# One pool of eight PSUM banks in place of a pool of three and a pool of five, in a one-core decoder layer

## The chip, the cores and the metric

The kernel runs on one core of one Trainium2 chip. The metric is the device time of one execution in microseconds. Before the change it was measured three times: 2459.76, 2463.95 and 2460.2 us, a median of 2460.2 us. One more execution was recorded by the hardware profiler; the profile and every answer of the trace come from that one.

The engines are named as in the profile: PE is TensorE's matmul (PEld its weight load), DVE is VectorE, ACT is ScalarE, POOL is GpSimd, SP is SyncE, which issues most DMAs.

## The reference, cut to what matters

One decoder layer over a prompt of 2048 tokens and 8 single-token samples, model width 1024, in float32:

```
mod  = silu(c) @ w_ada + b_ada                      # shift, scale, gate, twice
h    = rmsnorm(x, g_mix) * (1 + scale_m) + shift_m
q, k, v, g_ret, x_lru, g_lru = split(h @ w_in)      # 3072 columns
ret  = silu(g_ret) * groupnorm(retention(rotary(q), rotary(k), v))   # 4 heads of 128
lru  = rg_lru(causal_conv4(x_lru)) * gelu(g_lru)    # 512 channels
x    = x + gate_m * (concat(ret, lru) @ w_out)
h    = rmsnorm(x, g_ffn) * (1 + scale_f) + shift_f
u    = causal_conv3(h @ w_up_conv)                  # 2816 columns
x    = x + gate_f * ((gelu(u) * (h @ w_up_gate)) @ w_down)
y    = rmsnorm(x, g_final)
```

Beside y, the new states of the retention, of the RG-LRU and of both convolutions are returned, for the prompt and for the samples.

## The kernel before, in words

**Groups and blocks.** The 2056 columns (tokens) are worked off in three groups of 688, 680 and 688, each cut into two blocks of 344 or 340 columns. Activations lie with the channel on the partition and the token along the row. A group runs through the whole layer before the next one's large products begin; at the seam between two groups the final norm of the one and the load and first norm of the other run side by side.

**Large products.** Every float32 product is made from a high and a low part in three matmuls (`mm3`, lines 373 to 375: high x high, high x low, low x high), all into one tile of PSUM. PSUM has eight banks in this program, and a tile takes one bank of 512 float32. Three kinds of large product exist:

- `proj` (line 605): a column block of `w_in` times the normed input, 24 matmuls into one tile. `head_item` then reads the tile with VectorE (the rotary turn, lines 622 to 624) or with ScalarE, `lru_x` and `lru_g` with ScalarE.
- `down_item` (line 845): `w_out` or `w_down`. Of `w_down` one tile takes the contributions of two feature tiles, that is six matmuls, and the last two pairs are done together with twelve. VectorE's line 851 reads the tile and adds it, times the gate, to `x`.
- `quad_item` (with `product`): the two up-projections by a scheme of seven products for a 2 x 2 block matrix (`PRODUCTS`, P1 to P7). A family of seven products uses up to three tiles, called x, z and y (`qx`, `qz`, `qy` in the profile); products of one family accumulate into the same tile after ScalarE's or VectorE's copy of what stood there before (`keep`, line 1016, high priority). In the first three pairs y comes from the pool of the large products, everything else from the other one.

**Small products.** Transposes of the input (`xT`) and of the output (`yT`, line 1118), the retention's chunks (`kvT`, `o`, `oT`), the gates of the RG-LRU (`zr`, `zi`), the modulation (`ada`) and the norms' broadcasts (`bc`, `bc2`, `z`). In `final`, a chunk of up to 128 tokens takes two `yT` tiles; ScalarE squares them (line 1120), and VectorE scales them into the output (line 1130) once the norm is known.

**Weights.** A block of weights is fetched raw, split into high and low (ScalarE line 303, POOL or VectorE line 304), and written back to memory in the first group; later groups fetch the finished parts. For the up-projections VectorE also forms sums of blocks (line 357), in the first group only. Eight blocks of weights can be held.

**What sets the order.** The program is written as a list of items in the order of need (`group_items`), with two queues of side work: `soon` (norms, RG-LRU chains, final norm) and `bg` (retention), of which a step is emitted after an item. The build then hands all of it to a planner that runs a simulated clock (`_TC`): at each engine the ready instruction with the earliest place in the program goes next, `high_priority` moves a place forward. A tile gets its bank when its first writer is placed, and an instruction that finds no bank free in its pool is left waiting while later ones go ahead. So the banks that a pool has take part in deciding the order on every engine.

**The pools of PSUM.** Pool `pm` (line 111) has three banks (`PM`, line 34) and is reached by `psm`; pool `pt` (line 112) has the other five and is reached by `pst`. From `pm` come `proj`, `down`, the early `qy`, the first group's `bc` and a few output transposes at the very end; from `pt` comes the rest.

Of the kernel before, what the change touches and what calls it, by code (L numbers as in the profile page):

```python
# [10 lines left out]
F32 = mybir.dt.float32  # L11
# [5 lines left out]
P = 128  # L17
# [13 lines left out]
WIDE, HASTE = 9, 200  # L31
SPLIT = (2, 5)
FIRST = 4
PM = 3
LAGB, LAG = 1, 2


# [61 lines left out]
def hybrid_step(ctx: ExitStack, tc: tile.TileContext, I, O):  # L99
# [8 lines left out]
    tp = ctx.enter_context(tc.tile_pool(name="t", bufs=10))  # L108
    sp = ctx.enter_context(tc.tile_pool(name="s", bufs=3))
    dp = ctx.enter_context(tc.tile_pool(name="d", bufs=1, space=bass.MemoryType.DRAM))  # L110
    pm = ctx.enter_context(tc.tile_pool(name="pm", bufs=PM, space=bass.MemoryType.PSUM))
    pt = ctx.enter_context(tc.tile_pool(name="pt", bufs=8 - PM, space=bass.MemoryType.PSUM))

    def ctile(cols, name, dt=F32):
        return con.tile([P, cols], dt, tag=name, name=name)
# [2 lines left out]
        return tp.tile([P, BMAX + 4], F32, tag="t", name=name)  # L118

    def psm(name):  # L120
        return pm.tile([P, 512], F32, tag="m", name=name)

    def pst(name):
        return pt.tile([P, 512], F32, tag="t", name=name)

    def slot(name, dt=F32):
        return xp.tile([P, 4, TMAX], dt, tag="x", name=name)
# [29 lines left out]
    V.memset(cT, 0.0)  # L157
    cTv = cT.rearrange("p (k b) -> p k b", b=32)
    ps = pst("c_ps")
    T.transpose(ps[:, 0:72], crow[0:72, :], ident[0:72, 0:72])  # L160
    th = tiny(72, "cth")
# [25 lines left out]
    def load_rows(i, t_):  # L187
        col = sum(n for g in stage[:i] for _, n in g)
        r = sum(n for _, n in stage[i])
        q = pst("rows_ps")  # L190
        T.transpose(q[:, 0:r], t_[0:r, :], ident[0:r, 0:r])
        S.activation(out=vec[:, col:col + r], in_=q[:, 0:r], func=AF.Copy)
# [186 lines left out]
    def ada_mm(j, k):  # L379
        if k == 0:  # L380
            ada_ps[j] = pst("ada")
        ada_acc(ada_ps[j], units.pop(("w_ada", j, k)), k)
        if k == KC - 1:
            ada_finish([(j, 0)], ada_ps[j])
# [89 lines left out]
    class Group:  # L474
# [83 lines left out]
        def norm1(g, b, how):  # L558
            bc = pst("bc") if g.gi else psm("bc")
            for i, (c0, w) in enumerate(g.pieces):  # L560
                a0, a1 = max(c0, b[0]), min(c0 + w, b[1])
                if a0 < a1:
                    dg = tiny(P, "dg")
                    V.tensor_scalar(out=dg[0:w, 0:a1 - a0], in0=ident[0:w, a0 - c0:a1 - c0],
                                    scalar1=g.r1[i][0:w, 0:1], scalar2=None, op0=ALU.mult)
                    T.matmul(bc[:, a0 - b[0]:a1 - b[0]], ones[0:w, :], dg[0:w, 0:a1 - a0],
                             start=True, stop=True)
            yield
            yield from g.hnorm(b, bc, 1, 0, how)
# [33 lines left out]
        def proj(g, unit, b):  # L603
            n = b[1] - b[0]
            q = psm("proj")
            for k in range(KC):
                mm3(q[:, 0:n], *unit[k], g.hh[k // 4][:, k % 4, b[0]:b[1]], g.hl[k // 4][:, k % 4, b[0]:b[1]],
                    k == 0, k == KC - 1)
            return q[:, 0:n]
# [232 lines left out]
        def down_item(g, keys, parts, jg, b, m):  # L842

            np_, n = g.npr(b), b[1] - b[0]
            q = psm("down")
            for i, key in enumerate(keys):
                wh, wl = (v[:, m % 4, :] for v in units[key])
                xh, xl = parts[i][b]
                mm3(q[:, 0:n], wh, wl, xh, xl, i == 0, i == len(keys) - 1)
            xs = g.xk(m)[:, b[0]:b[0] + np_]  # L850
            V.scalar_tensor_tensor(out=xs, in0=q[:, 0:np_], scalar=modv[:, jg, m, 0:1], in1=xs,  # L851
                                   op0=ALU.mult, op1=ALU.add)
            if np_ < n:
                if (jg, m) not in g.started:
                    g.started.add((jg, m))
                    V.tensor_copy(fsv[:, m, :], q[:, np_:n])
                else:
                    V.tensor_tensor(out=fsv[:, m, :], in0=fsv[:, m, :], in1=q[:, np_:n], op=ALU.add)
# [594 lines left out]
```

## Time and profile before

| What | us |
|---|---|
| median of three runs | 2460.2 |
| the profiled execution | 2463.86 |
| its span, first to last instruction | 2462.1 |
| PE busy in the span | 2359.8 (96%) |
| PEld busy | 2275.5 (92%) |
| DVE busy | 1452.9 (59%) |
| ACT busy | 869.6 (35%) |
| POOL busy | 716.9 (29%) |
| mean granted TensorE clock | 0.988 |

Matmuls overlap: each is shown with some 0.32 us, though one starts about every 0.16 us. A stretch without holes shows PE and PEld busy all the time, so the idle time before an instruction, and what ended it, says more than the busy share. In the view of waits a row reads: the engine and tile that waited, the instruction that ended the wait, then the total in us, the number of times, and the longest.

### The profile page before, as it was taken

How to read it: one execution, taken by the hardware profiler on the slowest of the kernel's cores; microseconds unless marked ns; L12 is line 12 of the kernel's file. 1: busy time of each engine (PE TensorE's matmuls, PEld its weight loads, DVE VectorE, ACT ScalarE, POOL GpSimd, SP SyncE). 2: the span in 40 equal slices, each digit the busy share in tenths (PEclk: the TensorE clock that was granted, in tenths of full speed). 3: DMA queues.
4: the chain of work that ended last, by engine and by line, in shares of the span. 5: the costliest groups of instructions: out<-in, count | busy, mean ns of one | idle time of the engine just before them, and what ended most of it. 6: DMA issues, size and time to landing. Idle time of an engine off the chain costs nothing.

```text
span 2462.1 us, 40114 instructions
## 1 busy us (share of the span) xinstructions
PE 2359.8 (96%) x15157; PEld 2275.5 (92%) x15157; DVE 1452.9 (59%) x3181; ACT 869.6 (35%) x1964; POOL 716.9 (29%) x739
## 2 busy tenths in 40 slices
PE   5999998999999999999899999999999989999998
PEld 4987797999999999999899999999999989999998
DVE  5646777875766665666754444446667675444444
ACT  4323554544444444243422222243124241222222
POOL 3444440257666743243001010112222210101011
PEclk9999999999999999999999999999999999999999
DMA  9476655878878875343566666666442465666674
GB/s 299 163 261 223 210 172 190 305 276 287 304 285 304 323 251 184 120 157 139 189 222 235 222 238 220 241 213 215 139 130 96 145 231 199 239 220 234 219 252 160
DMA packets 243493, 536.04 MB, mean 218 GB/s; under 512 B 19223, under 2 KB 114055, under 8 KB 243292
## 3 DMA queue, kind: packets, MB, share of 16 engines
q1 hardware_dynamic: 242220, 532.01, 62.6%
q8 instruction: 120, 1.97, 0.3%
q10 hardware_dynamic: 696, 0.91, 0.1%
q0 software_dynamic: 384, 0.56, 0.1%
q14 instruction: 73, 0.60, 0.1%
HBM read 385.10 MB, written 148.42 MB: 217 GB/s over the span
## 4 chain that ended last, share of the span: by engine, by line
PE 53%; DVE 4%; ACT 2%; DMA 1%; issue 1%; POOL 1%; POOLq 0%; SPq 0%; ACTq 0%; DVEq 0%
PE down L374 6%; PE down L373 6%; PE down L375 6%; PE qx L374 4%; PE qx L375 4%; PE qx L373 4%; PE proj L373 3%; PE proj L375 3%; PE proj L374 3%; PE qz L373 2%; PE qz L374 2%; PE qz L375 2%; PE qy L374 1%; PE qy L373 1%; PE qy L375 1%
## 5 line engine op out<-in xcount | busy, mean ns | idle before, releaser
L851 DVE SCALAR_TENSOR_TENSOR x<-down,mod,x 128x344 f32<-128x344 f32 (+2 forms) x624 | 349.0, 569 | 347.0 <-PE down L375 342.3
L373 PE MATMUL proj<-hh,wb 128*128 128x344 f32 (+1 forms) x1152 | 378.5, 329 | 14.3 <-DVE h L580 6.0
L375 PE MATMUL proj<-hh,wb 128*128 128x344 f32 (+1 forms) x1152 | 373.6, 325 | 2.7 <-POOL wb L304 2.5
L374 PE MATMUL proj<-hl,wb 128*128 128x344 f32 (+1 forms) x1152 | 372.5, 323 | 0.0
L458 POOL TENSOR_TENSOR ffl<-cv,ffh 128x344 fp32r<-128x344 f32 (+1 forms) x120 | 124.7, 1046 | 782.0 <-ACT ffh L457 736.7
L374 PE MATMUL qx<-op,wb 128*128 128x344 f32 (+1 forms) x1020 | 325.5, 319 | 2.6 <-DVE op L921 2.6
L373 PE MATMUL qx<-op,wb 128*128 128x344 f32 (+1 forms) x1020 | 324.7, 320 | 1.2 <-ACT op L920 1.2
L375 PE MATMUL qx<-op,wb 128*128 128x344 f32 (+1 forms) x1020 | 324.5, 319 | 0.0
L373 PE MATMUL down<-ffh,wb 128*128 128x344 f32 (+1 forms) x960 | 304.7, 324 | 7.6 <-DVE x L851 7.4
L375 PE MATMUL down<-ffh,wb 128*128 128x344 f32 (+1 forms) x960 | 306.4, 319 | 0.0
L374 PE MATMUL down<-ffl,wb 128*128 128x344 f32 (+1 forms) x960 | 306.3, 319 | 0.0
L304 POOL TENSOR_TENSOR wb<-wr,wb 128x512 fp32r<-128x512 f32 x164 | 223.9, 1376 | 230.7 <-ACT wb L303 222.1
L373 PEld LDWEIGHTS proj<-hh,wb 128*128 128x128 f32 x1152 | 218.4, 190 | 25.9 <-issue 9.5
L375 PEld LDWEIGHTS proj<-hh,wb 128*128 128x128 f32 x1152 | 218.7, 190 | 5.7 <-POOL wb L304 3.9
L374 PEld LDWEIGHTS proj<-hl,wb 128*128 128x128 f32 x1152 | 219.1, 190 | 3.3 <-POOL hl L588 0.9
L1076 DVE SCALAR_TENSOR_TENSOR cv<-u,vec,cv 128x344 f32<-128x344 f32 (+2 forms) x264 | 170.8, 665 | 50.6 <-ACT cv L1056 48.1
L374 PEld LDWEIGHTS qx<-op,wb 128*128 128x128 f32 x1020 | 191.7, 188 | 3.4 <-DVE op L921 3.4
L373 PEld LDWEIGHTS qx<-op,wb 128*128 128x128 f32 x1020 | 191.5, 188 | 2.0 <-ACT op L920 1.8
L373 PEld LDWEIGHTS down<-ffh,wb 128*128 128x128 f32 x960 | 179.3, 188 | 14.3 <-DVE x L851 13.7
L375 PEld LDWEIGHTS qx<-op,wb 128*128 128x128 f32 x1020 | 191.4, 188 | 0.0
L373 PE MATMUL qz<-op,wb 128*128 128x344 f32 (+1 forms) x528 | 169.7, 325 | 14.6 <-ACT op L920 10.7
L375 PEld LDWEIGHTS down<-ffh,wb 128*128 128x128 f32 x960 | 180.6, 188 | 0.0
(314 smaller groups left out, 4952.1 us busy)
## 6 DMA issues: line engine op xcount, KB each, us to landing
wb<-w_down SPq DMA_DIRECT2D x100, 512.0 KB
wb<-w_up_conv_S SPq DMA_DIRECT2D x92, 512.0 KB
wb<-w_up_gate_S SPq DMA_DIRECT2D x92, 512.0 KB
wb<-w_in SPq DMA_DIRECT2D x72, 512.0 KB
wb<-w_up_conv_A SPq DMA_DIRECT2D x69, 512.0 KB
wb<-w_up_gate_A SPq DMA_DIRECT2D x69, 512.0 KB
w_in<-wb SPq DMA_DIRECT2D x48, 512.0 KB
w_up_conv_S<-wb SPq DMA_DIRECT2D x44, 512.0 KB
```

Source lines behind the costliest of these rows:

```text
L304: lo_on.tensor_tensor(out=w[:, 512:1024], in0=src, in1=w[:, 0:512].bitcast(F32), op=ALU.subtract)
L373: T.matmul(out, wh, xh, start=first, stop=False, skip_group_check=more)
L374: T.matmul(out, wh, xl, start=False, stop=False, skip_group_check=more)
L375: T.matmul(out, wl, xh, start=False, stop=last, skip_group_check=more)
L458: G.tensor_tensor(out=lo[:, 0:n], in0=src, in1=hi[:, 0:n].bitcast(F32), op=ALU.subtract)
L851: V.scalar_tensor_tensor(out=xs, in0=q[:, 0:np_], scalar=modv[:, jg, m, 0:1], in1=xs, op0=ALU.mult, op1=ALU.add)
L1076: V.scalar_tensor_tensor(out=cv[:, 0:np_], in0=u[:, j:j + np_], scalar=cfw[:, j, ft:ft + 1], in1=cv[:, 0:np_], op0=ALU.mult, op1=ALU.add)
```

## The change

The two pools of PSUM become one pool of eight banks. `psm` and `pst` remain as names, and both take a tile from that pool, under one tag. Which tile uses which of the two names is as before, and nothing else in the program differs.

```diff
-PM = 3
...
-    pm = ctx.enter_context(tc.tile_pool(name="pm", bufs=PM, space=bass.MemoryType.PSUM))
-    pt = ctx.enter_context(tc.tile_pool(name="pt", bufs=8 - PM, space=bass.MemoryType.PSUM))
+    pb = ctx.enter_context(tc.tile_pool(name="pb", bufs=8, space=bass.MemoryType.PSUM))
...
     def psm(name):
-        return pm.tile([P, 512], F32, tag="m", name=name)
+        return pb.tile([P, 512], F32, tag="b", name=name)
 
     def pst(name):
-        return pt.tile([P, 512], F32, tag="t", name=name)
+        return pb.tile([P, 512], F32, tag="b", name=name)
```

## The prediction

> **What bounds the kernel now.** The page came first, for the engines over the whole span.
>
> ```profile
> span 2462.1 us, 40114 instructions
> PE 2359.8 (96%) x15157; PEld 2275.5 (92%) x15157; DVE 1452.9 (59%) x3181; ACT 869.6 (35%) x1964; POOL 716.9 (29%) x739
> ```
>
> TensorE sets the time: no other engine is above 59%, and what the change can win has to come out of the share in which TensorE has no work it may start. Matmul times overlap, so the weight loads (PEld) show the holes better. Which stage has them is read from the stage table, a row for each stretch: the feed-forward of the first token group (580 to 860 us), the seam behind it, the feed-forward of the second group, the next seam, the feed-forward of the third, and the tail.
>
> ```profile
> 580.00:860.00 280.00, 272.46 (x1705) 266.28 (x1704) 186.72 (x266) 130.36 (x298) 189.08 (x144) 1.00 0.82 299
> 860.00:930.00 70.00, 66.71 (x436) 64.58 (x435) 39.34 (x79) 29.39 (x73) 26.74 (x28) 0.98 0.75 267
> ...
> 1210.00:1620.00 410.00, 405.39 (x2592) 404.33 (x2592) 190.05 (x367) 114.22 (x298) 41.03 (x41) 1.00 0.67 232
> 1620.00:1700.00 80.00, 75.84 (x500) 74.39 (x500) 43.43 (x95) 28.24 (x68) 19.06 (x22) 0.98 0.63 218
> ...
> 1990.00:2400.00 410.00, 405.72 (x2567) 404.50 (x2566) 207.73 (x516) 112.90 (x294) 40.32 (x40) 1.00 0.65 226
> 2400.00:2463.00 63.00, 51.30 (x340) 49.86 (x338) 28.05 (x78) 15.79 (x41) 8.73 (x10) 0.92 0.46 160
> ```
>
> After the stretch's length stand PE, PEld, DVE, ACT and POOL busy, then granted clock, DMA share and GB/s. The second and third groups' feed-forward is almost closed: weight loads busy 404.33 and 404.50 of 410 us. The first group's is not: 266.28 of 280, so 13.7 us are open, about 5%, at full clock, with DVE busy only 67% and POOL 68%. From the third group's row comes the price of a matmul, 410 / 2567 = 0.16 us from start to start.
>
> The waits of TensorE's weight loads over the whole span (total, times, longest) name who ends these holes.
>
> ```profile
> PEld down L373 <- DVE x L851: 15.2, 25, 1.9
> PEld qz L373 <- ACT op L920: 11.2, 3, 6.5
> ...
> PEld proj L373 <- DVE rotb L624: 5.7, 4, 2.1
> PEld qy L373 <- ACT p L1016: 4.9, 3, 2.0
> PEld qz L373 <- ACT p L1016: 4.4, 3, 2.4
> ...
> PEld yT L1118 <- DVE y L1130: 2.7, 5, 1.1
> ```
>
> A `down` product doesn't use the `x` that L851 writes. What it needs of L851 is that this instruction has read an older `down` tile out of its bank. So the first row is waiting for a free bank, and likewise `proj` behind L624 (the last reader of an older projection) and `yT` behind L1130. The sum of these three is 15.2 + 5.7 + 2.7 = 23.6 us, 1% of the span: all that the change can win at first hand. The rows with L1016 look alike and are not: the second product accumulates into the very tile that L1016 copies out, so it waits for its own tile, and no number of banks ends that (9.3 us). The row with L920 waits for operands (11.2 us).
>
> The same view for 480 to 860 us alone puts 12.8 of the 15.2 us into the first group's feed-forward:
>
> ```profile
> PEld down L373 <- DVE x L851: 12.8, 20, 1.9
> ```
>
> One such place, first VectorE in order of time, then the weight loads that waited:
>
> ```profile
> 668.09 1.05 DVE L851 SCALAR_TENSOR_TENSOR x<-down,mod,x 128x344 f32<-128x344 f32 x2
> 670.15 4.70 DVE L1076 SCALAR_TENSOR_TENSOR cv<-u,vec,cv 128x344 f32<-128x344 f32 x4 [1.02 <-ACT cv L1056]
> 674.78 0.56 DVE L851 SCALAR_TENSOR_TENSOR x<-down,mod,x 128x344 f32<-128x344 f32 x1
> 675.27 1.29 DVE L357 TENSOR_TENSOR ws<-wr 128x512 f32<-128x512 f32 x1
> 676.48 0.57 DVE L851 SCALAR_TENSOR_TENSOR x<-down,mod,x 128x344 f32<-128x344 f32 x1
> 676.97 1.28 DVE L357 TENSOR_TENSOR ws<-ws,wr 128x512 f32<-128x512 f32 x1
> 678.17 1.53 DVE L851 SCALAR_TENSOR_TENSOR x<-down,mod,x 128x344 f32<-128x344 f32 x3
> ```
>
> ```profile
> 675.39 0.19 PEld L373 LDWEIGHTS down<-ffh,wb 128*128 128x128 f32 x1 [0.67 <-DVE x L851]
> 677.10 0.19 PEld L373 LDWEIGHTS down<-ffh,wb 128*128 128x128 f32 x1 [0.62 <-DVE x L851]
> 678.79 0.19 PEld L373 LDWEIGHTS down<-ffh,wb 128*128 128x128 f32 x1 [0.45 <-DVE x L851]
> ```
>
> From 669.1 to 674.8 VectorE empties no bank, and then only one between two sums for the weight operands (L357, 1.29 us). A `down` of six matmuls takes TensorE 6 x 0.16 = 0.96 us, so three are quickly done, and the three banks of their pool are full. The L357 sums are made for the first group only; later groups fetch finished operands, which is why only this stage shows the hole again and again.
>
> **The change part by part.** No instruction is added or removed: the matmuls, the evictions and the DMAs are the same ones. Two things change: which banks a tile may get, and, since the planner places instructions and banks together, the order on every engine.
>
> *More banks for `down` in the first group.* The code gives one product family the banks x, z and y, and y is short-lived; the next family's x may already be open. So the other pool's five hold two or three tiles here, at most four, and with eight in one pool four to six are left for `down` in place of three. In the place quoted the fourth, fifth and sixth `down` wait 0.67 + 0.62 + 0.45 = 1.74 us. With five banks the fourth starts 0.67 us earlier, at 674.7, the fifth 0.96 us behind it, and the sixth, at 676.6 at the earliest, takes the bank that is free from 674.78 + 0.56 = 675.3 on: no wait is left. With four banks the fourth alone is rid of its wait, and the two behind it take what is left over. So between 0.67 and 1.74 of 1.74 us goes, 39% to 100%; for the stage's 12.8 us that is 5 to 12.8. I take 11, near the upper end, since four tiles at once in the other pool are the exception. VectorE has room to deliver (67% busy). Late next would be the weight blocks: the DMA share is 0.82 in this stage, and the same transfers in 369 us in place of 380 make it 0.84, still below full.
>
> *The seams between groups.* Here the long-held tiles are the transposed outputs `yT`, each bank held until L1130 has read it. This is what the 1640 to 1700 stretch shows of `yT`, and 1660 to 1700 of `proj`:
>
> ```profile
> L1118 PE MATMUL yT<-cst,x x48: 270/272/310, 1647.4 to 1682.7; 128*128 128x128 f32 x32, 128*84 128x128 f32 x16
> ...
> L1130 DVE SCALAR_TENSOR_TENSOR y<-yT,ssf,gfin x12: 737/742/751, 1673.9 to 1692.4; 128x512 f32<-128x512 f32 x8, 84x512 f32<-84x512 f32 x4
> ```
>
> ```profile
> L373 PE MATMUL proj<-hh,wb x57: 316/321/422, 1667.9 to 1699.7; 128*128 128x344 f32 x57
> ...
> L622 DVE TENSOR_TENSOR head<-proj,rope x4: 497/505/517, 1682.9 to 1688.7; 128x344 f32<-128x344 f32 x4
> ```
>
> The first `yT` is written at 1647.4 and not read out before 1673.9, so banks stand full for up to 26.5 us. Before, `yT` can take five banks at most, and three stay for `down` and `proj`. After, twelve `yT` tiles and the projections draw from the same eight. A projection bank is worth 24 x 0.16 = 3.8 us of work, a `yT` bank only four short transposes. One bank more for the projections ends the two short waits (5.7 + 2.7 = 8.4 us over the whole span, an upper bound for the gain). One bank fewer costs 3.8 us at each of two seams, 7.6 us in all. The direction isn't in this trace; I take a gain of 1 us, near the middle of +8.4 and -7.6.
>
> *The new order elsewhere.* The second and third feed-forwards have no bank wait to lose, and 5.5 us of 410 open each: nothing to win, and a worse order could only cost. The retention stages wait for operands, not banks. I cost both at 0, hidden behind a PE queue that is full there; if that cover fails, the nearest row is the operand wait of 11.2 us, and the sum gets worse by a part of it. Bounds: +/- 5 us.
>
> *Sum.* 11 + 1 + 0 = 12 us less. The profiled execution took 2463.86 us around a span of 2462.1, 3.7 us above the median of 2460.2; 2463.86 - 12 = 2451.9, and at the level of the median 2448.
>
> [...]
>
> **The rivals.**
>
> *Crowding: slower.* Tiles with a long life take the banks that the pool of three kept for the large products. The mechanism sits at the two seams: all six `yT` tiles of the first block are written early and keep six of eight banks until 1673.9 and later, so two are left for `down` and `proj`. A single bank beyond the two is 3.8 us; if the projections have one bank in place of three until VectorE gets to L622 at 1682.9, TensorE stands from about 1671.7 (1667.9 + 3.8) to 1682.9, 11.2 us at each seam, 22.4 in all. With the 12 us won elsewhere that makes 2460.2 + 22.4 - 12 = 2470.6. It decides from the point where more than six us are lost at each seam. For it speaks the 26.5 us of holding; against it, that the projections at the seam wait for VectorE in any case, and that the planner sees the banks and can put other work first. [...]
>
> *No difference.* The planner fills every bank it is given. If it lets `down` and the next family run further ahead until eight banks are as tight as three and five were, the 20 waits come back at other tiles, and the time is 2458 to 2462. For it: bank and order come from one simulated clock, and a plan that leaves VectorE no time to spare turns every delay on the chip into a wait, however many banks there are. Against it: the 5.6 us without an eviction cover fewer than six `down` tiles, so the wait has an end. That the change does nothing because there are eight banks before and after gives the same time, 2460; the 20 waits behind three full banks, with others free, speak against that.
>
> *All of it.* Seams and feed-forward both lose their bank waits: 2460.2 - 23.6 = 2437.
>
> **How the numbers follow.** Forecast (most of the feed-forward's waits gone, the seams about even): 0.48, its own range 2440 to 2455. All of it: 0.12. No difference: 0.18. Crowding: 0.22. The range takes the lower end from the rival "all of it", 2437, and reaches up to crowding's 2470. What a measurement here can tell from no change is about 0.2%, 4.9 us, so faster is below 2455.3: 0.48 + 0.12 = 0.60; same 0.18; slower 0.22.
>
> **What would show it.** In the waits of the weight loads, `down` behind L851 should fall from 15.2 to under 5 us; in the stage table, the first feed-forward should take some 10 us less and its weight loads be busy above 98%. The seam should have `proj` behind L624 no longer than now; if instead `proj` or `down` waits there for L1130, it is crowding. The forecast is wrong if `down` keeps its 20 waits, if new waits for banks appear at qx, qz or qy, or if operand waits (L920, L580) grow because the order has moved.

## The result and the profile after

The changed kernel takes 2481.4 us (median; 2479.11 to 2485.77) against 2461.7 us for the kernel before in the same comparison: a ratio of 1.0087, 95% interval 1.0073 to 1.0101. It is about 20 us slower, where 12 us less had been forecast, and outside the range.

The page of the profiled execution after (2481.57 us, with a span of 2479.8):

```profile
span 2479.8 us, 40187 instructions
PE 2358.3 (95%) x15157; PEld 2284.2 (92%) x15157; DVE 1443.6 (58%) x3181; ACT 863.5 (35%) x1958; POOL 711.8 (29%) x739
```

The work is the same, but TensorE is held up for longer, and in other places. In the stage table, the first group's feed-forward has weight loads busy 271.64 of 280 us, against 266.28 before:

```profile
580.00:860.00 280.00, 273.67 (x1738) 271.64 (x1737) 176.82 (x263) 133.77 (x307) 190.01 (x145) 0.99 0.86 314
```

The feed-forward ends earlier now, and this stretch holds some of the seam. Up to the last `qx` (841 us, 853 before) the weight loads are busy 259.24 of 261 us, against 261.54 of 273: the stage is closed.

Where time is won and lost is read from two tiles that mark the stages: `proj` (the stage with retention and RG-LRU, called the mixing stage here) and `qx` (the feed-forward). Each row gives the shortest, median and longest matmul in ns and the start of the first and of the last one in us, for group one, two and three. Before, `proj` and then `qx`:

```profile
L373 PE MATMUL proj<-hh,wb x384: 313/321/627, 30.8 to 344.7; 128*128 128x344 f32 x192
L373 PE MATMUL proj<-hh,wb x384: 312/319/651, 888.7 to 1149.1; 128*128 128x340 f32 x192
L373 PE MATMUL proj<-hh,wb x384: 313/321/582, 1667.9 to 1929.1; 128*128 128x344 f32 x192
L373 PE MATMUL qx<-op,wb x340: 313/319/429, 395.7 to 853.0; 128*128 128x344 f32 x170
L373 PE MATMUL qx<-op,wb x340: 312/317/422, 1195.8 to 1630.9; 128*128 128x340 f32 x170
L373 PE MATMUL qx<-op,wb x340: 313/319/424, 1981.2 to 2417.2; 128*128 128x344 f32 x170
```

After (two lines are gone from the file, so the first of the three matmuls is line 371 and every later line is two less):

```profile
L371 PE MATMUL proj<-hh,wb x384: 313/321/995, 48.0 to 347.6; 128*128 128x344 f32 x192
L371 PE MATMUL proj<-hh,wb x384: 312/319/983, 881.3 to 1149.2; 128*128 128x340 f32 x192
L371 PE MATMUL proj<-hh,wb x384: 313/321/994, 1665.2 to 1945.4; 128*128 128x344 f32 x192
L371 PE MATMUL qx<-op,wb x340: 313/319/634, 398.4 to 841.0; 128*128 128x344 f32 x170
L371 PE MATMUL qx<-op,wb x340: 312/317/632, 1196.9 to 1633.4; 128*128 128x340 f32 x170
L371 PE MATMUL qx<-op,wb x340: 313/319/634, 1999.6 to 2439.6; 128*128 128x344 f32 x170
```

From last start to last start, after against before:

| From one mark to the next | change, us | running total, us |
|---|---|---|
| start to the last `proj` of group 1 | +2.9 | +2.9 |
| to the last `qx` of group 1 (feed-forward) | -14.9 | -12.0 |
| to the last `proj` of group 2 (seam, mixing) | +12.1 | +0.1 |
| to the last `qx` of group 2 | +2.4 | +2.5 |
| to the last `proj` of group 3 (seam, mixing) | +13.8 | +16.3 |
| to the last `qx` of group 3 | +6.1 | +22.4 |
| to the end | -4.7 | +17.7 |

So the forecast gain was made, 14.9 us up to the end of the first feed-forward, and then given back twice over, mostly in the stages with many small products. The first `proj` of a group, also in the lines, roughly divides a seam from the mixing stage behind it (the last transposes of a seam run on past it): the two seams change by +4.6 and -5.2 us, the two mixing stages by +7.5 and +19.0. The waits of the weight loads over the whole span say on what. Before, in the rows of the small products:

```profile
PEld kvT L674 <- DVE sT L647: 3.8, 4, 2.1
...
PEld bc L888 <- DVE sq L877: 1.3, 1, 1.3
...
PEld oT L674 <- DVE on L471: 0.7, 2, 0.4
PEld os L756 <- issue: 0.6, 3, 0.2
```

After:

```profile
PEld bc L886 <- DVE sq L875: 13.2, 5, 7.5
PEld kvT L672 <- DVE sT L645: 10.3, 10, 2.4
PEld oT L672 <- DVE on L469: 10.3, 13, 2.0
...
PEld bc L886 <- issue: 7.0, 1, 7.0
...
PEld yT L1116 <- DVE y L1128: 5.7, 5, 3.7
...
PEld os L754 <- issue: 5.3, 2, 3.0
...
PEld yT L1116 <- DVE rotb L622: 4.3, 2, 2.4
```

The row of `down` behind the eviction (15.2 us before) is gone, and so is that of `proj` behind the rotary turn (5.7). In their place TensorE waits for the operands of small products: retention's transposes (kvT, oT), the samples' output (os), the second norm's sums (bc). None of these four is a wait for a bank. The two rows of `yT` are (L1128 and L622 read older tiles), but they make 10.0 us, where the waits for banks made 23.6 before.

One such place in the third group, TensorE in order of time, after:

```profile
1771.34 0.32 PE L373 MATMUL down<-mlh,wb 128*128 128x344 f32 x1
1773.68 0.46 PE L754 MATMUL os<-vts,sTs 8*128 8x128 f32 x2 [2.02 <-DVE sTs L742]
1774.07 0.62 PE L757 MATMUL os<-sret,qm 128*2 128x128 f32 x16
1774.62 0.43 PE L371 MATMUL down<-mrh,wb 128*128 128x344 f32 x1
```

TensorE stands 2 us in front of `os`, whose operand comes late from VectorE. Directly behind it runs a `down` product from the finished parts of earlier heads. In the kernel before, the same two products stood the other way round, `down` first, and `os` found its operand ready:

```profile
1769.83 0.32 PE L375 MATMUL down<-mlh,wb 128*128 128x344 f32 x1
1770.08 0.48 PE L756 MATMUL os<-vts,sTs 8*128 8x128 f32 x2
```

The order of the built programs shows why. In every kernel of this study, a pool hands out its tiles strictly in the order in which the program asks for them: no tile is first written before an earlier one of the same pool. With two pools, 444 of the 1310 PSUM tiles begin after a later tile of the other pool has begun. With one pool, none does. The pool is not only a number of banks, it is a queue: a small tile that waits for its operands holds up each later large one, and the planner can put less work between a small product and what it depends on. Counted along TensorE's order (0.157 us a large matmul, 0.11 a small one, from start to start in the two traces), the mean work between a product and the one from which its operands come:

```
              tiles        o     oT    os    zr    bc2 sums   (us of TensorE work)
              overtaken
before        444          6.1   5.7   7.2   6.4   5.5
after           0          4.0   3.6   3.1   4.5   2.3
```

So the work that can cover an operand which comes late has shrunk by 30% and more. That the planner's clock has these operands ready in time, and VectorE on the chip is a little later, would explain why the planner accepts this order; no run compares the two.

Beside the holes, the clock itself was lower. The mean granted clock of TensorE fell from 0.988 to 0.980. In the record of the granted clock in the two traces it stands at one half for 62 us before and 99 us after; from 60 us on (in the 60 us ahead of that, weight loads are busy for only 24.45 us before and 24.25 after), matmuls run for 42 and 65 us of that. In these stretches the large ones start about 0.29 us apart (median), outside them 0.157, so nearly half of such time is lost, and the lower clock costs the changed kernel some 11 us more than the kernel before (an estimate from these figures).

### The profile page after: what moved, and what is told of

Same layout as the page of the kernel before. It is cut to its first block, busy times and chain, and to the rows that moved or that the text cites. A ratio compares the mean times of both kernels' runs of the same rounds, so it can differ in the third digit from the quotient of the medians.

```text
span 2479.8 us, 40187 instructions
## 1 busy us (share of the span) xinstructions
PE 2358.3 (95%) x15157; PEld 2284.2 (92%) x15157; DVE 1443.6 (58%) x3181; ACT 863.5 (35%) x1958; POOL 711.8 (29%) x739
## 4 chain that ended last, share of the span: by engine, by line
PE 73%; DVE 11%; DMA 7%; issue 3%; POOL 2%; ACT 2%; SPq 1%; POOLq 0%; DVEq 0%; ACTq 0%
PE down L371 8%; PE down L373 8%; PE down L372 8%; PE proj L371 6%; PE proj L373 6%; PE proj L372 6%; PE qx L371 5%; PE qx L372 5%; PE qx L373 5%; PE qz L371 3%; PE qz L372 3%; PE qz L373 3%; DMA xt<-in_x_prompt 2%; PE qy L371 1%; PE qy L372 1%
## 5 line engine op out<-in xcount | busy, mean ns | idle before, releaser
L849 DVE SCALAR_TENSOR_TENSOR x<-down,mod,x 128x344 f32<-128x344 f32 (+2 forms) x624 | 343.5, 567 | 299.2 <-PE down L373 296.9
L301 ACT ACTIVATE wb<-wr 128x512 fp32r<-128x512 f32 x206 | 126.2, 626 | 161.9 <-DMA wr<-in_w_in 50.4
L372 PEld LDWEIGHTS down<-ffl,wb 128*128 128x128 f32 x960 | 180.7, 188 | 0.0
```

The lines of the kernel that those rows point to most:

```text
L301: S.activation(out=w[:, 0:512], in_=src, func=AF.Copy)
L372: T.matmul(out, wh, xl, start=False, stop=False, skip_group_check=more)
```

## The experiments

Three theories stood against each other. Queue: the one order of a single pool costs the time. Crowding (the rival of the prediction): long-held tiles leave too few banks. Scatter: each change makes the planner deal a new order, good or bad by chance. All times are medians of repeated runs, with ratios to the kernel before on the same chip.

**The gain alone.** Two pools of three and five; only `down` of the first group's feed-forward takes turns:

```diff
-            q = psm("down")
+            q = (pst if jg == 5 and g.gi == 0 and m % 2 else psm)("down")
```

> Two pools of three and five as before; only the first group's `down` products of w_down take their tile from the two pools in turn (odd m from the pool of five). This is the larger supply of banks for `down` alone. Queue theory (a pool hands out its tiles strictly in the order of the program, so one pool for everything is one queue in which a small product that waits for its operands holds up every later tile): the stages with retention and RG-LRU stay as before, each within 2 us, and the stretch from 480 to 860 us gets 10 to 13 us shorter; 2448 to 2453 against 2461.7. Crowding theory (banks are short because long-held tiles take them): `down` now takes banks from the families' tiles, so qx, qz or qy wait for banks instead, and less than 5 us is won; 2457 or more. Scatter theory (any change makes the planner deal a new order, good or bad by chance): anything within 10 us, and the retention stages differ from before.

Measured: 2450.3 us against 2462.3, ratio 0.995 (0.9933 to 0.9967). The stages' marks are the last `qx` of group 1 and the last `proj` of group 2 and 3:

```profile
L373 PE MATMUL qx<-op,wb x340: 313/319/427, 395.2 to 842.4; 128*128 128x344 f32 x170
...
L373 PE MATMUL proj<-hh,wb x384: 312/319/651, 874.1 to 1136.3; 128*128 128x340 f32 x192
...
L373 PE MATMUL proj<-hh,wb x384: 313/321/653, 1653.2 to 1916.7; 128*128 128x344 f32 x192
```

At these marks it is 10.6, 12.8 and 12.4 us ahead of the kernel before: the gain arises in the first feed-forward and is kept from there on. The forecast's working for this stage holds, size included: from the last `proj` of group 1 (345.7 here) to its last `qx` the stretch is 11.6 us shorter.

**One bank fewer in the one pool.**

```diff
-    pb = ctx.enter_context(tc.tile_pool(name="pb", bufs=8, space=bass.MemoryType.PSUM))
+    pb = ctx.enter_context(tc.tile_pool(name="pb", bufs=7, space=bass.MemoryType.PSUM))
```

> The changed kernel with one pool of seven banks in place of eight. Queue theory: the order of the tiles is the same, and banks were not what the mixing stages waited for, so 2479 to 2486 against 2481.4 of the changed kernel, with the same waits of kvT, oT, os and bc for their operands; at most a few us more in the first group's feed-forward. Crowding theory: one bank fewer costs a projection's 3.8 us at each of two seams and more in the first feed-forward, 2489 or more, with `down` and `proj` waiting behind the last readers of older tiles. Scatter theory: no forecast.

Measured: 2480.1 us, ratio 1.0073 (1.0058 to 1.0088), as with eight banks. The waits of small products for their operands are those of the changed kernel:

```profile
PEld oT L672 <- DVE on L469: 13.6, 13, 3.2
PEld bc L886 <- DVE sq L875: 13.2, 5, 7.5
PEld yT L1116 <- DVE y L1128: 11.9, 9, 4.1
...
PEld kvT L672 <- DVE sT L645: 8.9, 8, 2.4
```

The wait for banks at `yT` has doubled (11.9 us for 5.7), and yet the kernel is no slower. Taking a bank away costs nothing that can be measured, so a lack of banks doesn't explain the 20 us.

**Seven banks in two pools.** The counterpart of the last one: as many banks, but two queues.

```diff
-    pt = ctx.enter_context(tc.tile_pool(name="pt", bufs=8 - PM, space=bass.MemoryType.PSUM))
+    pt = ctx.enter_context(tc.tile_pool(name="pt", bufs=7 - PM, space=bass.MemoryType.PSUM))
...
-                    q = (psm if u == 0 and i else pst)("yT")
+                    q = (psm if len(qs) < 3 else pst)("yT")
```

> Two pools as before, of three and four banks: seven in all, as in the kernel with one pool of seven (2480.1). In the very last norm three output transposes come from the pool of three, so that its seven tiles fit. Queue theory (in one pool a tile that waits holds up all later ones; in two pools the other one goes on): close to the kernel before, 2460 to 2468 against 2462.3, with no long waits of oT, os or bc for operands, though there is one bank fewer than in the changed kernel. Theory that the loss comes from the number of banks that each kind may use: 2470 or more, since both kinds have fewer than in the pool of eight. Scatter theory (each plan is good or bad by chance): anywhere from 2450 to 2485.

Measured: 2460.8 us, ratio 0.999 (0.998 to 1.0). With the same seven banks, two pools are 19 us faster than one. `down` waits for its banks as in the kernel before, and the small products hardly wait:

```profile
PEld down L373 <- DVE x L851: 16.2, 30, 1.5
...
PEld oT L674 <- DVE on L471: 2.3, 2, 1.3
...
PEld bc L888 <- DVE sq L877: 1.3, 1, 1.3
```

This pair of runs settles the cause between one shared pool and the number of banks. In the order of the program, 444 tiles are overtaken here, as before, and the work ahead of o, oT, os, zr and the sums of bc2 is 6.2, 5.6, 7.2, 6.4 and 5.5 us.

**Four and four.**

```diff
-PM = 3
+PM = 4
...
-                    q = (psm if u == 0 and i else pst)("yT")
+                    q = (psm if len(qs) < 4 else pst)("yT")
```

> Two pools of four banks each. Queue theory: the order is as free as before, and `down` has one bank more, so about half of the 12 us that e1_down_both won: 2452 to 2460. Theory that scarce banks of the small tiles gave the order its slack: with four instead of five for them still more slack, so also no slower than 2462. Scatter theory: anywhere from 2450 to 2485.

Measured: 2444.2 us, ratio 0.9913 (0.9898 to 0.9927): faster than the kernel before and the changed one, and by more than the theory gave. The marks are 18.0 us ahead at the last `qx` of group 1 (835.0) and 22.4 at the last `proj` of group 3 (1906.7). The wait of `down` for banks is 0.4 us, so one bank more is enough to end it. Why this kernel gains some 6 us more than the one with turns for `down` wasn't taken apart.

**Retention's outputs and the second norm in a queue of their own.** One pool of seven, and one bank for o, oT, os and bc2:

```diff
-    pb = ctx.enter_context(tc.tile_pool(name="pb", bufs=8, space=bass.MemoryType.PSUM))
+    pb = ctx.enter_context(tc.tile_pool(name="pb", bufs=7, space=bass.MemoryType.PSUM))
+    pr = ctx.enter_context(tc.tile_pool(name="pr", bufs=1, space=bass.MemoryType.PSUM))
...
-                    o = pst("o")
+                    o = psr("o")
```

> Seven banks in one pool, and the eighth as a pool of its own for the small tiles o, oT, os and bc2 (retention's outputs and the second norm). So these have a queue of their own, though with one bank only, and everything else has one bank fewer. Queue theory: the waits of oT, os and bc for operands (10.3, 7 and 20 us of weight-load idle time in the changed kernel) mostly go, those of kvT and zr stay: 2455 to 2470. Crowding theory: banks are scarcer than in any other kernel here, one of them bound to few tiles: slower than the changed kernel, 2485 or more. Scatter theory: no forecast.

Measured: 2480.7 us, ratio 1.0074 (1.0059 to 1.0089). The forecast of 2455 to 2470 fell. The waits that were to go did go (oT 2.9 us in place of 10.3, os 0.7 in place of 5.3), but others came:

```profile
PEld yT L1120 <- DVE y L1132: 11.6, 8, 4.2
PEld qz L375 <- ACT u L1062: 11.3, 2, 5.7
PEld xT L519 <- issue: 10.3, 5, 3.4
...
PEld qz L375 <- issue: 7.3, 1, 7.3
```

The rows of `yT` and `xT` are much like those with one pool of seven (11.9 and 9.6 us), and those of qz stand at the second norm, in place of bc. By the marks, the stretches up to the last `proj` of each group are 13.9 us shorter in all than with one pool of seven, and those behind them up to the last `qx` 13.2 us longer. Whether time was saved and lost again, or only put off, isn't shown.

**The second norm alone.** The same with `bc2` as the only tile in the pool of one bank (`bc = psr("bc2")`; o, oT and os stay in the pool of seven).

> Seven banks in one pool, and the eighth as a pool of its own for bc2 alone (six tiles of 1310: the second norm's sums and broadcast). Queue theory: TensorE no longer stands before the sums (20 us of weight-load idle time in the changed kernel, in three places), since products of the first block may go ahead of them; but it then stands at the next thing that this norm feeds, the first qz, as the kernel before does (11 us), so 5 to 12 us are won: 2470 to 2477. If nothing but the number of banks mattered: as with one pool of seven, 2481 or more.

Measured: 2485.6 us, ratio 1.0092 (1.0075 to 1.0108). This forecast fell too. TensorE no longer stands before the sums, and stands before qz instead:

```profile
PEld qz L375 <- issue: 13.7, 2, 7.3
...
PEld qz L375 <- ACT u L1062: 5.6, 1, 5.6
```

The two rows make 19.3 us, in the same three places, against the 20.2 us of the two rows of bc in the changed kernel: the norm's chain sets the time there, and what TensorE does in it is only named differently. In the kernel before, the same norm shows as 11.2 us at qz (behind L920) and 1.3 at bc. So at most some 8 of the 20 us can be a price of the change, and theories that add up rows of waits, this one included, overstate what lifting one of them brings.

**Large and small, cut cleanly.** Five banks for `proj`, `down` and all tiles of the product families, three for the small tiles:

```diff
-PM = 3
+PM = 5
...
-                          psm if bank == "y" and i < 3 else pst)
+                          psm)
...
-                    q = (psm if u == 0 and i else pst)("yT")
+                    q = (psm if len(qs) < 5 else pst)("yT")
```

> Two pools cut in another way: five banks for proj, down and all tiles of the product families (qx, qy, qz), three for all small tiles. Eight banks, two queues; what is large shares one. Queue theory: retention, RG-LRU and the second norm run beside the large products as before, so no long waits of oT, os and bc; the feed-forward stages have no small tiles, so one queue costs nothing there, and `down` has two to three banks as before: 2450 to 2465. If the number of banks for small tiles mattered (three in place of five, or eight): the mixing stages lose, 2470 or more. Scatter theory: anywhere from 2450 to 2485.

Measured: 2471.5 us, ratio 1.0029 (1.0017 to 1.0041): outside the 2450 to 2465 of the queue theory, and just inside the rival's "2470 or more". The waits of oT, os and bc stay away, but the families now share five banks and one queue with `down`, and their y waits for them:

```profile
PEld qy L373 <- DVE u L1055: 19.1, 3, 7.2
...
PEld qy L373 <- DVE x L851: 8.2, 7, 3.6
```

The three waits of the first row stand at the start of the three feed-forwards, where the kernel before waits 11.2 us for the second norm, so only some 8 of the 19.1 us are new. With the second row that still speaks against "one queue costs nothing there"; whether the one queue or the number of banks is at fault, this run doesn't separate. Nor do the mixing stages come off free: up to the last `proj` of group 1 it is 6.7 us behind the kernel before, and retention's `o` waits 9.1 us for its operand in place of 1.9. Whether three banks are too few for the small tiles isn't shown.

**Tiles moved across, from four and four.** Three kernels start from the fastest one and move one kind of tile into the other queue. First, the projections into the queue of the small tiles:

```diff
-            q = psm("proj")
+            q = pst("proj")
```

> Two pools of four (f2_four_four, 2444.2), but the projections `proj` take their tiles from the pool of the small tiles. Four banks each as there, and `down` keeps its four. Queue theory: while retention and RG-LRU run, a projection that is ready must now begin behind every earlier small tile, as in the one pool; the work between a small product and the product that its operands come from is again some 4.5 us in place of 6 to 7 in the order of the program (o 4.6 for 6.1, oT 4.2 for 6.0, zr 4.5 for 7.2). So waits of kvT, oT, o and zr for operands come up in the three mixing stages, 10 us or more in all: 2454 to 2468. If only the number of banks counted: `down` has its four banks alone, so no slower than 2444 to 2450.

Measured: 2520.5 us, ratio 1.0243 (1.0226 to 1.026), 76 us slower than four and four. (These three were measured on another chip; by the ratios the distances to four and four are 81 us here, and 7 and 14 us for the two below.) The direction is right, the size was far too small. Beside the operand waits there are now real waits for banks, since nearly everything of the mixing stages and seams shares four:

```profile
PEld yT L1118 <- DVE y L1130: 17.6, 10, 2.3
PEld oT L674 <- issue: 14.6, 2, 8.1
PEld kvT L674 <- DVE sT L647: 12.8, 8, 2.6
```

Second, `bc2` into the queue of the large tiles (`bc = psm("bc2")`).

> Two pools of four (f2_four_four, 2444.2), but the second norm's tile bc2 comes from the pool of the large tiles: the first product of a family must not begin before the norm's sums. Queue theory with what e4_bc2_ring showed: TensorE stands before bc in place of standing before qz, the norm's chain sets the time in both, so within 4 us of 2444: 2441 to 2449. If the wait before bc were a loss of its own (13 to 20 us in the changed kernel): 2455 or more.

Measured: 2446.5 us, ratio 0.994 (0.9925 to 0.9955), within 4 us of four and four as expected, though not by the ratios. Third, retention's o and the samples' os into that queue (`o = psm("o")`, `o = psm("os")`).

> Two pools of four (f2_four_four, 2444.2), but retention's o and the samples' os come from the pool of the large tiles: 76 of 1310 tiles stand in the other queue, so that projections and `down` tiles may not pass them. Queue theory: o and os wait for operands in front of ready large products, oT and zr as in f2; some 5 us: 2447 to 2456, and less than g1_proj_small loses. If only the number of banks counted: the small tiles have more room, no slower than 2446.

Measured: 2453.7 us, ratio 0.9968 (0.9954 to 0.9982): 9.5 us for 76 tiles out of 1310 that stand in the other queue, with the number of banks unchanged. The waits of kvT show it:

```profile
PEld kvT L674 <- DVE sT L647: 11.8, 12, 3.1
```

Scatter alone doesn't give this picture: six changed kernels whose order between large and small tiles was free, or nearly so, lie between 2444 and 2472 us, and all five kernels in which nearly all large and small products share one pool, or the projections stand among the small tiles, between 2480 and 2521. But within the two sets the times still differ by 27 and 40 us, and not all of that is accounted for, so chance in the planner's order may have a share of some us.

## Why the prediction was wrong

*What bounds the kernel, and the waits for banks*: right. The 15.2 us of `down` were bank waits; they vanish in the changed kernel, and nearly so at four and four (0.4 us).

*More banks for `down`, 11 us*: right. From the last `proj` to the last `qx` of group 1 it was 11.6 us in e1_down_both, and alone it makes the kernel 12 us faster. In the changed kernel it was 14.9 us, 2.1 above the upper bound, so something beside these waits changed there too. That weight blocks would be late next didn't come true in this stage.

*The seams, a gain of 1 us with bounds of +8.4 and -7.6*: about right. Divided at the first `proj`, one seam is 4.6 us longer and the other 5.2 us shorter, a gain of 0.6 us in all.

*The new order elsewhere, cost at 0, "hidden behind a PE queue that is full there", bounds +/- 5 us*: this step failed. What it put at 0 measured 37.9 us: 2.9, 7.5 and 19.0 in the three mixing stages (the first with the start of the kernel) and 2.4 and 6.1 in the second and third feed-forward. It took the order as something that the change shakes a little. In fact one pool makes it a different rule: large and small products may no longer pass each other. That "the retention stages wait for operands, not banks" was true, and it was the reason to look there, not to leave them out: what hid those operands' delay was large work that could go first, and the change took part of that cover away. The prediction did name growing operand waits as a sign of being wrong, but without a price. The text ahead of it says that an instruction without a bank waits "while later ones go ahead"; it left out that, of these, the ones that begin a new tile come from the other pool only, which the order of the program before would have shown.

*Crowding, 2470.6*: it had the right sign and about half the size, by the wrong mechanism. With seven banks in one pool the time is the same, and with seven in two pools the loss is gone. Its price rested on projections that stand still for 11.2 us at each seam for want of banks, and the matmuls of `proj` wait only 1.3 us, once, for a bank that `yT` held.

*All of it, 2437*: it didn't happen. The kernel before has eight banks in use too, three and five. With all eight open to every tile the kernel is 0.9% slower, and seven banks in two pools are as fast as eight were. The measurement decides: in a kernel like this, which tiles share a queue matters more than the last bank.

*The price of a hole, counted at its length* (11.2 us at each seam in crowding): too low. In the changed kernel TensorE stood for 7.25 us ahead of bc in group 1, from 388.5 to 395.8 us, and from 393.0 to 403.2 the granted clock was 0.50. Matmuls ran for 7.4 of these 10.2 us, so some 3.4 us were lost beside the hole (an estimate from the 0.157 and 0.29 us from start to start). At the two seams before, the granted clock was 0.98, and the longest wait of a matmul 2.2 us. The 0.92 of the tail is a clock of 0.50 from 2453.3 us on, and the last matmul ends at 2452.9, so nothing is left there to slow down.

What stays open: how the 20 us divide among the coupled kinds, and between the holes and the lower clock. The kernels that freed one kind at a time (e3_second_ring, e4_bc2_ring) only moved the waits.

## What to carry to other kernels

A pool of tiles with a ring of buffers is also a queue: put products that wait for long chains and products that are always ready into different pools, even at the price of a bank, and count as a cost of merging pools all work that could pass before. A wait row tells where an engine stands, not what is won when it goes; look first for what sets the time behind it. If one class of tiles is short of banks, lend it some (e1_down_both) or shift the split (four and four, 2444.2 us), and leave the queues apart. Where to cut has to be tried: a cut by size alone (f3_large_small) was 0.3% slower.

## What was not expected of the hardware

A hole of 2.0 us in TensorE's work was followed by a granted clock of 0.51 for 3.4 us. The hole is the wait for `os` shown above; the stretch just ahead of the hole, and the one that begins 1.7 us behind it, read (length, PE and PEld busy with counts, other engines, then the granted clock):

```profile
1769.00:1771.50 2.50, 2.50 (x17) 2.37 (x16) 2.38 (x10) 0.00 (x0) 0.00 (x0) 1.00 0.00 0
1775.40:1778.80 3.40, 3.40 (x14) 3.40 (x13) 1.47 (x3) 0.00 (x0) 0.70 (x2) 0.51 0.53 159
```

In the second stretch 14 matmuls took the time of nearly 22 (at 0.157 us each), so the low clock cost about another 1.2 us (an estimate from these numbers); in the 3.2 us after that it was 1.00 again. No other place in TensorE's work from 1768 to 1783 us is idle. The traces before and after have more such places. From 60 us on, and while matmuls still run, the record of the granted clock has 12 stretches at one half in the trace before and 15 in the trace after, 44 and 75 us in all, and in the 7 us ahead of each TensorE was idle for 1.4 us or more. In these two traces, a half-clock stretch began in the hole or up to 5.2 us behind it in 16 of 20 holes of 2 us or more, and in 17 of 56 of 0.7 to 2 us. So in these traces low clock and holes go together, the more often the longer the hole; that the hole is the cause is the author's guess, since no run varies one hole alone.
